# Hybrid encoder block: fourteen places for the expert weights instead of ten, and the last gate's weights sent through them

## The chip, the cores and the metric

The kernel runs on one core of a Trainium2 chip. The metric is the device time of one execution in microseconds (us). Engines are named as in the profile: PE (TensorE, matrix products), PEld (its weight loads), DVE (VectorE), ACT (ScalarE), POOL (GpSimd) and SP (SyncE, which here only issues transfers). MB in the text is 1,048,576 bytes, the size of one weight tile.

## What is computed

One layer of an encoder over 512 tokens of width 1024, all in float32. First a mixer of four branches with gates; then a mixture of 16 experts, in which each expert chooses 64 tokens; then a gate with an embedding; then a norm:

```
x = mixer_sublayer(x, ...)                       # four branches, gates, w_br, output projection w_out
x = x + expert_choice_ffn(rmsnorm(x, norm2_g), w_router, w_e_gate, w_e_up, w_e_down)
gate = sigmoid(rmsnorm(x, norm3_g) @ w_ple_gate)
x = x + gate * (p @ w_ple_proj)
return rmsnorm(x, final_g)

# expert e, on its 64 tokens xe
ye = (silu(xe @ w_gate[e]) * (xe @ w_up[e])) @ w_down[e]     # times the affinity, added to the tokens' rows
```

An expert's weights are 12 MB (gate and up 8 MB, down 4 MB), 192 MB for all; w_ple_gate is 4 MB.

## The kernel before

The program is one long list of instructions for each engine. It has four stretches: the branches with their gates, the output projection, the routing (eight rounds of a maximum search, and a gather of each expert's rows), and the experts with the last gate.

**Experts.** `up(e)` does eight steps k of four matmuls on the tile with the gate and up weights of k (L1213); then the activation (`gated`, L1216 and L1217); `hidden` transposes the result; `down(e)` does eight steps with the down weights, two steps to a tile (L1230). The order of PE is written out: after every second expert `spread` adds the results of a pair of experts to the tokens' rows X (L1255 to L1258), and a pair's rows are fetched (`fetch`, L1159) and transposed (`turn`). Experts 2 and 3 also carry parts of the embedding's projection (`project`, L1281), expert 12 the collection of the rows of the last two experts (`gather`). Tokens' results of experts 14 and 15 are finished apart.

**The last gate.** `base(i, k0, k1)` (four calls i of eight steps k) multiplies the tokens' rows with w_ple_gate. It does so in split precision: `gsplit(k, h)` makes from a 128x512 piece of the weights a rounded part gh on ACT and the rest gl on DVE (both through `parts`, L1092 and L1093), and PE takes six matmuls from them (L408 to L410). There are two buffers each for gh and gl, so step k+2 is split only when PE has left step k. `finish_gate` takes the same weights, not split, for the rows of experts 14 and 15.

**Places for weights.** A tile of 128 x 2048 numbers (1 MB) is given a place by `place()`: in rotation three of the pool `ring` (which held the weights of the earlier stretches) and seven of the pool `big`, which exists from the end of the output projection. The weights w_ple_gate have eight tiles `WG` of their own of 0.5 MB, loaded before the experts (L1087) and multiplied at once with the norm's gain g3 on ACT (L1088). Expert 0's down weights and the first step of expert 1 go to small tiles (`we`, 0.25 MB), which lie in the space of other, not yet needed buffers (the tags "x", "y" and "m").

All weights are issued by SP from one queue, in one order. SP waits with a transfer until PE has left the place's tile before, and everything behind it waits too. The lists below name a tile by `w`, whichever pool it is from.

Of the kernel before, what the change touches and what calls it, by code (L numbers as in the profile page):

```python
# [8 lines left out]
F32 = mybir.dt.float32  # L9
# [9 lines left out]
D = 1024  # L19
# [16 lines left out]
BIG = 14  # L36
# [7 lines left out]
KS = 4  # L44
WARM = 4
SOLO = (14, 15)
NEARLY = 8
FAR = 4096.0
SM = {}

# [155 lines left out]
def _body(ctx, tc, nc, A, out):  # L206
# [19 lines left out]
    def S(name, i=0):  # L226
        o, n = SM[name]
        return sm[:, o + i:o + i + 1]
# [53 lines left out]
    def YT(name, dt=F32R):  # L282
        return mpool.tile([128, 512], dt, name=name, tag="y", bufs=8)
# [609 lines left out]
    iap = xr.tile([128, 8], F32, name="iap")  # L893
    iai = xr.tile([128, 8], I32, name="iai")
    wr = xr.tile([128, 8, 16], F32, name="wr")
    wo = ctxR.enter_context(tc.tile_pool(name="wo", bufs=8, side="right", reuse_waits="tile"))

    def load_out(half):
# [29 lines left out]
    same = xl.tile([128, 64], F32, name="same")  # L928
    one = xl.tile([128, 128], F32, name="one")
    e6 = [xl.tile([128, 64], F32, name=f"e6{i}") for i in range(2)]  # L930
    WG = [xl.tile([128, D], F32, name=f"WG{k}") for k in range(8)]
    zp = ctx.enter_context(tc.tile_pool(name="zp", bufs=4, reuse_waits="tile"))
    h2d = dram.tile([T, D], F32, name="h2d")

# [88 lines left out]
                              ident.rearrange("p (c r) -> p r c", r=8)[:, 4 * h:4 * h + 4], start=True, stop=True)  # L1023
    ctxR.close()

    big = ctx.enter_context(tc.tile_pool(name="big", bufs=BIG // 2, side="right", reuse_waits="tile"))

    vals = xe[0:64, 256:384]
    idx = xe[0:64, 384:448].bitcast(U32)
# [53 lines left out]
    dve.tensor_copy(dsti[1], dst[1])  # L1083


    for k in range(8):
        sp.dma_start(WG[k], A["w_ple_gate"][k])  # L1087
        act.activation(WG[k], WG[k], AF.Copy, scale=S("g3", k))  # L1088

    def parts(hi, lo, v, eng=dve):  # L1090

        act.copy(hi, v)  # L1092
        eng.tensor_sub(lo, v, hi.bitcast(F32))  # L1093

    def xpart(b, i):

# [3 lines left out]
        xps[b, i] = MT("xTh", F32R), YT("xTl")  # L1100
        parts(*xps[b, i], p)

    nsplit = 0

    def gsplit(k, h, eng=dve):
        nonlocal nsplit
        if nsplit < 2:
            gh_.append((MT if nsplit else XH)("gh", F32R))
            gl_.append((MT if nsplit else XH)("gl", F32R))
        hi, lo = gh_[nsplit % 2], gl_[nsplit % 2]  # L1110
        nsplit += 1
        parts(hi, lo, WG[k][:, h * 512:(h + 1) * 512], eng)
        return hi, lo

    xps, Z, zb = {}, [], {}

    def base(i, k0, k1):
        bp, h = divmod(i, 2)
        if k0 == 0:
            zb[i] = [ps("b"), ps("b")]  # L1120
            if h == 0:
                z = place()
                Z.extend([z[:, 0:1024], z[:, 1024:2048]])
        for k in range(k0, k1):
            gh, gl = gsplit(k, h)
            for j in range(2):
                hi, lo = xps[2 * bp + j, k // 4]
                t = slice((k % 4) * 128, (k % 4 + 1) * 128)
                mm3(zb[i][j], hi[:, t], lo[:, t], gh, gl, k == 0, k == 7)
        if k1 == 8:  # L1130
            for j in range(2):
                act.copy(Z[2 * bp + j][:, h * 512:(h + 1) * 512], zb[i][j])
# [4 lines left out]
    n_w = 0  # L1137

    def place():
        nonlocal n_w  # L1140
        n_w += 1
        if n_w % (BIG // 2 + 3) < 3:
            t = ring.tile([128, 2048], F32, name="w", tag="w")
        else:
            t = big.tile([128, 2048], F32, name="w2", tag="w2")
        return t

    def wtile(src):
        t = place()
        sp.dma_start(t, src)  # L1150
        return t[:, 0:1024], t[:, 1024:2048]
# [23 lines left out]
    def halves(t):  # L1175
        return [t[:, 0:512], t[:, 512:1024]]

    def early(k):
# [4 lines left out]
            return [YT("we", F32), YT("we", F32)]  # L1183
        return [MT("we"), MT("we")]

    def load(e):
        wg, wu, wd = [], [], []
        for k in range(8):
            if e == 1 and k == 0:
                for i, w in enumerate((wg, wu)):  # L1190
                    w.append([YT("we", F32) for h in range(2)])
                    for h in range(2):
                        c = i * 1024 + h * 512
                        sp.dma_start(w[0][h], A["w_gu"][e, k, :, c:c + 512])
            else:
                for w, t in zip((wg, wu), wtile(A["w_gu"][e, k])):
                    w.append(halves(t))
        for k in range(8):
            if e == 0 and k < NEARLY:
                wd.append(early(k))  # L1200
                for h in range(2):
                    c = (k % 2) * 1024 + h * 512
                    sp.dma_start(wd[k][h], A["w_dn"][e, k // 2, :, c:c + 512])
            elif k % 2 == 0:
                wd.extend(halves(w) for w in wtile(A["w_dn"][e, k // 2]))
        return wg, wu, wd

    def up_part(e, xts, w2, acc, k0, k1):
# [75 lines left out]

    def project_rows():

        pg = MT("pg")
# [73 lines left out]
    def row_rstd(a, tag):  # L1361
# [3 lines left out]
            pe.matmul(q[:, 0:1], one, a[:, i:i + 1], start=i == 0, stop=i == 1)  # L1365
        return rstd(q[:, 0:1], 1.0 / D, tag=tag)


    def finish_start(x_, xgT, junk):

        for i in range(2):
            p = ps("t")
            s = slice(i * 256, (i + 1) * 256)
            for k in range(2 * i, 2 * i + 2):
                pe.transpose(p[:, k * 128:(k + 1) * 128], x_[:, k * 128:(k + 1) * 128], ident)
            act.copy(xgT[:, s], p[:, s])
        return row_sums(x_, "u", junk)

    def finish_factor(a):
# [63 lines left out]
    for b in range(2):  # L1443
        xpart(b, 0)
    up_part(14, xts, (wg, wu), acc, 2, 8)
    gated(acc)
    for b in range(2):
        xpart(b, 1)
    base(0, 0, 4)
# [106 lines left out]
```

## Time and profile before

| | us |
|---|---|
| median of 3 runs (range) | 1086.66 (1085.18 to 1088.04) |
| the profiled execution | 1086.17 |
| its span | 1084.4 |
| PE busy | 1004.5 (93%) |
| DVE, ACT busy | 482.3, 341.7 |
| mean granted PE clock | 0.982 of full speed |
| read from memory | 258.88 MB (10^6 bytes) |

The span is cut by the page into 40 slices of 27 us. PE is busy in tenths 8 to 9 nearly everywhere; around 520 to 548 us it waits for the routing. The weights' transfers keep the sixteen DMA engines full from about 520 us to about 1000 us; before that they are mostly idle.

### The profile page before, as it was taken

To read this page: it belongs to the slowest core of one execution; us is meant where nothing else is said; L and a number is where in the kernel's file an instruction comes from. 1 tells how busy PE (TensorE), PEld (TensorE's weight loads), DVE (VectorE), ACT (ScalarE), POOL (GpSimd) and SP (SyncE) were. 2 spreads that over 40 slices of the span, in tenths; PEclk is the share of its full clock that TensorE was granted. 3 is DMA by queue.
4 is the path that set the end of the run, shared out by engine and by line. 5 is a ranking of instruction groups with operands and counts; after the bars stand their busy time and mean duration, and the time that the engine had idled before them with its cause. 6 is when DMAs were issued, how large, how long until landed. Compare 5 with 4: busy or idle time off the path is not lost.

```text
span 1084.4 us, 12105 instructions
## 1 busy us (share of the span) xinstructions
PE 1004.5 (93%) x4566; PEld 597.4 (55%) x4566; DVE 482.3 (44%) x1078; ACT 341.7 (32%) x636; POOL 38.4 (4%) x45
## 2 busy tenths in 40 slices
PE   8999999999999999999489999988788898999996
PEld 5777887787668888878233333323232333336553
DVE  6996886555765556544600202011020203144646
ACT  6342335426553324362111111110101022134443
POOL 0022020000000000000000000000000000000001
PEclk9999999999999999999699999999999899999998
DMA  9222121411122532464998999999999999999401
GB/s 329 105 78 78 39 76 59 141 68 60 49 78 102 144 97 93 156 241 137 377 402 325 416 418 423 422 423 423 423 424 423 422 424 424 422 407 394 170 1 49
DMA packets 54259, 264.15 MB, mean 244 GB/s; under 512 B 6635, under 2 KB 11499, under 8 KB 30264
## 3 DMA queue, kind: packets, MB, share of 16 engines
q1 hardware_dynamic: 49840, 252.14, 58.8%
q0 software_dynamic: 1904, 6.44, 1.5%
q10 hardware_dynamic: 2456, 4.79, 1.4%
q8 instruction: 36, 0.59, 0.2%
q14 instruction: 23, 0.19, 0.1%
HBM read 258.88 MB, written 4.72 MB: 243 GB/s over the span
## 4 chain that ended last, share of the span: by engine, by line
PE 68%; DMA 15%; DVE 7%; issue 6%; ACT 3%; POOL 1%; POOLq 0%; SPq 0%; DVEq 0%; ACTq 0%
DMA w<-in_w_gu_dram 13%; PE ps_mm L1213 12%; PE ps_y L1230 8%; PE ps_mm L410 7%; PE ps_mm L409 7%; PE ps_mm L408 7%; PE ps_b L408 2%; PE ps_b L409 2%; PE ps_b L410 2%; PE ps_pj L408 2%; PE ps_pj L409 1%; PE ps_mm L990 1%; DVE X L1258 1%; PE ps_pj L410 1%; PE ps_mm L988 1%
## 5 line engine op out<-in xcount | busy, mean ns | idle before, releaser
L1213 PE MATMUL ps_mm<-w,xt 128*64 128x512 f32 x1016 | 230.8, 598 | 25.6 <-DMA w<-in_w_gu_dram 25.4
L1213 PEld LDWEIGHTS ps_mm<-w,xt 128*64 128x64 f32 x1016 | 70.8, 137 | 182.9 <-issue 121.3
L408 PE MATMUL ps_mm<-hhi,whi 128*128 128x512 f32 x392 | 156.7, 400 | 0.0
L410 PE MATMUL ps_mm<-hhi,wlo 128*128 128x512 f32 x392 | 155.2, 397 | 0.7 <-DVE wlo L325 0.5
L409 PE MATMUL ps_mm<-hlo,whi 128*128 128x512 f32 x392 | 154.9, 395 | 0.0
L1217 DVE TENSOR_TENSOR sg<-sg,ps_mm 128x512 f32<-128x512 f32 x16 | 11.0, 689 | 286.3 <-PE ps_mm L1213 286.3
L1230 PE MATMUL ps_y<-w,hd 128*64 128x512 f32 x480 | 109.2, 607 | 6.1 <-ACT hd L1238 6.1
L323 ACT CAST whi<-w 128x1024 fp32r<-128x1024 f32 x50 | 52.5, 1051 | 122.4 <-PE ps_mm L409 69.7
L408 PEld LDWEIGHTS ps_mm<-hhi,whi 128*128 128x128 f32 x392 | 74.1, 189 | 18.7 <-ACT whi L323 1.2
L410 PEld LDWEIGHTS ps_mm<-hhi,wlo 128*128 128x128 f32 x392 | 74.1, 189 | 18.7 <-issue 2.5
L409 PEld LDWEIGHTS ps_mm<-hlo,whi 128*128 128x128 f32 x392 | 74.0, 189 | 17.1 <-issue 2.5
L1216 ACT ACTIVATE sg<-ps_mm 128x512 f32<-128x512 f32 x16 | 9.6, 597 | 207.9 <-PE ps_mm L1213 207.9
L1230 PEld LDWEIGHTS ps_y<-w,hd 128*64 128x64 f32 x480 | 34.7, 139 | 70.8 <-issue 60.8
L325 DVE TENSOR_TENSOR wlo<-w,whi 128x1024 fp32r<-128x1024 f32 x49 | 60.1, 1230 | 5.9 <-ACT whi L323 5.8
L1248 ACT ACTIVATE ys<-ps_y,ia 64x512 f32<-64x512 f32 x28 | 19.1, 682 | 99.7 <-PE ps_y L1230 99.4
L1093 DVE TENSOR_TENSOR yh<-ys,yh 128x512 fp32r<-128x512 f32 x14 | 9.1, 688 | 76.2 <-ACT yh L1092 76.2
L621 DVE TENSOR_TENSOR sg<-ps_mm,rbs 128x512 f32<-128x512 f32 x32 | 22.1, 690 | 46.9 <-PE ps_mm L410 46.6
L1159 POOL DMA_INDIRECT xe<-h2d,iai x8 | 7.7, 966 | 712.3 <-DVE num L1081 373.4
L1093 DVE TENSOR_TENSOR gl<-WG,gh 128x512 fp32r<-128x512 f32 x32 | 22.1, 691 | 20.2 <-ACT gh L1092 20.2
L409 PE MATMUL ps_b<-gl,xTh 128*128 128x512 f32 x64 | 26.2, 410 | 0.6 <-DVE gl L1093 0.6
L1092 ACT CAST gh<-WG 128x512 fp32r<-128x512 f32 x32 | 19.9, 621 | 21.7 <-PE ps_b L410 15.5
L408 PE MATMUL ps_b<-gh,xTh 128*128 128x512 f32 x64 | 26.0, 406 | 0.0
(506 smaller groups left out, 1517.2 us busy)
## 6 DMA issues: line engine op xcount, KB each, us to landing
w<-in_w_gu_dram SPq DMA_DIRECT2D x127, 1024.0 KB, 19.2
w<-in_w_dn_dram SPq DMA_DIRECT2D x60, 1024.0 KB, 18.5
w<-in_w_in_dram SPq DMA_DIRECT2D x50, 512.0 KB, 4.1
wb<-in_w_br_dram SPq DMA_DIRECT2D x32, 128.0 KB, 2.2
w<-in_w_out_dram SPq DMA_DIRECT2D x8, 512.0 KB, 4.0
WG<-in_w_ple_gate_dram SPq DMA_DIRECT2D x8, 512.0 KB, 5.8
we<-in_w_dn_dram SPq DMA_DIRECT2D x16, 256.0 KB, 7.0
xk<-in_xT_dram SPq DMA_DIRECT2D x8, 256.0 KB, 3.9
```

Source lines behind the costliest of these rows:

```text
L323: act.copy(hi, raw)
L325: (pool if key in PW else dve).tensor_sub(lo, raw, hi.bitcast(F32))
L408: pe.matmul(p, whi, mhi, start=start, stop=False)
L409: pe.matmul(p, whi, mlo, start=False, stop=False)
L410: pe.matmul(p, wlo, mhi, start=False, stop=stop)
L621: dve.tensor_mul(g, p, rbs)
L1092: act.copy(hi, v)
L1093: eng.tensor_sub(lo, v, hi.bitcast(F32))
L1213: pe.matmul(t[h * 64:(h + 1) * 64], x, w[k][h], start=k == 0, stop=k == 7)
L1217: dve.tensor_mul(sg, sg, acc[1])
L1230: pe.matmul(y[h * 64:(h + 1) * 64], lt[:, k % 4, k // 4, :], w[k][h], start=n == 0, stop=n == 7)
L1248: act.activation(ys[h][r], y[hs], AF.Copy, scale=ia[hs, 16 + e:17 + e])
```

## The change

It makes fourteen places of ten. The eight WG tiles go; in their space lie four places (pool `wgp`). Of the seven places of `big` three become a pool `soon`, which is laid between the tokens' rows and the output projection's weights, in space that is free from the end of the branches; the other four stay in `big`. `place()` goes round all fourteen: wgp 0 to 3, ring 4 to 6, soon 7 to 9, big 10 to 13; a list TAIL gives the last ones by hand.

w_ple_gate is loaded as four tiles of 1 MB within expert 14's weights, between its up and its down weights. It is no longer multiplied by g3 beforehand: `gsplit` does it (an ACT activation with a scale for each row instead of a cast, and a DVE operation with that scale instead of a subtraction), and for the rows of experts 14 and 15 the transposed rows are multiplied instead (two DVE products in place of two ACT copies in `finish_start`). Two of expert 14's splits are made ahead of its activation.

Three more steps (2, k = 3, 4, 5) go to small tiles, as (1, 0) did, and the transfers after them are held behind them.

```diff
+AGAIN = {(1, 0): "y", (2, 3): "y", (2, 4): "m", (2, 5): "m"}
+N_ALL = 14 * 12 - 8 + 8 + 4
+TAIL = (4, 5, 6, 7) + (8,) + (9, 10, 11, 12, 13, 4, 5, 6) + (7, 9, 10, 11) + (12,)
+SOON = 3
...
+    soon = ctx.enter_context(tc.tile_pool(name="soon", bufs=SOON, side="right", reuse_waits="tile"))
     wo = ctxR.enter_context(tc.tile_pool(name="wo", bufs=8, side="right", reuse_waits="tile"))
...
-    WG = [xl.tile([128, D], F32, name=f"WG{k}") for k in range(8)]
+    wgp = ctx.enter_context(tc.tile_pool(name="wgp", bufs=4, reuse_waits="tile"))
...
-    big = ctx.enter_context(tc.tile_pool(name="big", bufs=BIG // 2, side="right", reuse_waits="tile"))
+    big = ctx.enter_context(tc.tile_pool(name="big", bufs=BIG // 2 - SOON, side="right", reuse_waits="tile"))
...
-    for k in range(8):
-        sp.dma_start(WG[k], A["w_ple_gate"][k])
-        act.activation(WG[k], WG[k], AF.Copy, scale=S("g3", k))
...
-        parts(hi, lo, WG[k][:, h * 512:(h + 1) * 512], eng)
-        return hi, lo
+        v = WG[k][:, h * 512:(h + 1) * 512]
+        i = act.activation(hi, v, AF.Copy, scale=S("g3", k))
+        dve.scalar_tensor_tensor(lo, v, S("g3", k), hi.bitcast(F32), op0=ALU.mult, op1=ALU.subtract)
+        return hi, lo, i
...
-        if n_w % (BIG // 2 + 3) < 3:
-            t = ring.tile([128, 2048], F32, name="w", tag="w")
-        else:
-            t = big.tile([128, 2048], F32, name="w2", tag="w2")
-        return t
+        pos = (n_w - 1) % 14 if n_w <= N_ALL else TAIL[n_w - N_ALL - 1]
+        if pos < 4:
+            return wgp.tile([128, 2048], F32, name="w3", tag="w3")
+        if pos < 7:
+            return ring.tile([128, 2048], F32, name="w", tag="w")
+        if pos < 7 + SOON:
+            return soon.tile([128, 2048], F32, name="w4", tag="w4")
+        return big.tile([128, 2048], F32, name="w2", tag="w2")
...
-            if e == 1 and k == 0:
+            if (e, k) in AGAIN:
+                T_ = YT if AGAIN[e, k] == "y" else MT
...
+        if e == 14:
+            for i in range(4):
+                t = place().rearrange("p (k d) -> p k d", k=2)
+                sp.dma_start(t, A["w_ple_gate"][2 * i:2 * i + 2].rearrange("k p d -> p k d"))
+                WG.extend([t[:, 0], t[:, 1]])
...
-            act.copy(xgT[:, s], p[:, s])
+            dve.tensor_mul(*(v[:, s].rearrange("p (a b c) -> p a b c", a=2, b=2) for v in (xgT, p)),
+                           g3[:, 2 * i:2 * i + 2].to_broadcast([128, 2, 2, 64]))
...
-    gated(acc)
+    ahead.extend(gsplit(k, 0) for k in range(2))
+    with tc.issue_after(ahead[1][2].ins):
+        gated(acc)
```

The first place is SP's queue after the output projection's weights (w_out). `w_gu` are gate and up weights, `w_dn` down weights. Before:

```order
L317 DMA w<-in_w_out_dram 128x1024 x7
L1150 DMA w<-in_w_gu_dram 128x2048
L1087 DMA WG_4116<-in_w_ple_gate_dram 128x1024
...
L1087 DMA WG_4123<-in_w_ple_gate_dram 128x1024
L1150 DMA w<-in_w_gu_dram 128x2048 x2
L1203 DMA we<-in_w_dn_dram 128x512 x4
L1194 DMA we<-in_w_gu_dram 128x512 x3
L1150 DMA w_4751<-in_w_gu_dram 128x2048
```

And now:

```order
L321 DMA w<-in_w_out_dram 128x1024 x7
L1157 DMA w<-in_w_gu_dram 128x2048
L1157 DMA w_4729<-in_w_gu_dram 128x2048
...
L1157 DMA w_4735<-in_w_gu_dram 128x2048
L1157 DMA w<-in_w_gu_dram 128x2048 x2
L1219 DMA we<-in_w_dn_dram 128x512 x4
L1204 DMA we<-in_w_gu_dram 128x512 x4
L1157 DMA w_4851<-in_w_gu_dram 128x2048
```

Where the eight gate tiles stood, four tiles of expert 0 stand. Three more tiles (expert 0's last step, expert 1's second and third) go out earlier still, on SP among the loads of the gates, behind the tokens' rows X. Before:

```order
L915 DMA X_3268<-in_x_dram 128x1x1024
L317 DMA w<-in_w_in_dram 128x1024
L612 DMA wb<-in_w_br_dram 128x256
L317 DMA w<-in_w_in_dram 128x1024
L612 DMA wb<-in_w_br_dram 128x256
```

And now:

```order
L920 DMA X_3268<-in_x_dram 128x1x1024
L1157 DMA w_4743<-in_w_gu_dram 128x2048
L616 DMA wb<-in_w_br_dram 128x256
L321 DMA w<-in_w_in_dram 128x1024 x2
L1157 DMA w_4847<-in_w_gu_dram 128x2048
L616 DMA wb<-in_w_br_dram 128x256
L1157 DMA w_4849<-in_w_gu_dram 128x2048
```

Three loads of 1 MB now stand between the gates' loads, which are otherwise as they were.

The second place is the end of SP's queue, from expert 14's last up tile on. Before, its down weights follow at once:

```order
L1150 DMA w_6456<-in_w_gu_dram 128x2048
L1150 DMA w<-in_w_gu_dram 128x2048 x2
L1150 DMA w<-in_w_dn_dram 128x2048
L1150 DMA w_6464<-in_w_dn_dram 128x2048
...
L1150 DMA w<-in_w_gu_dram 128x2048
L1150 DMA w_6798<-in_w_gu_dram 128x2048
```

Now the last gate's weights stand between, and expert 15's tiles behind them:

```order
L1157 DMA w_6460<-in_w_gu_dram 128x2048
L1212 DMA w_6462<-in_w_ple_gate_dram 128x2x1024
...
L1212 DMA w_6468<-in_w_ple_gate_dram 128x2x1024
L1157 DMA w<-in_w_dn_dram 128x2048 x3
L1157 DMA w_6476<-in_w_dn_dram 128x2048
L1157 DMA w_6806<-in_w_gu_dram 128x2048
```

So 4 MB have moved from before expert 0 to within expert 14; the order of PE among the experts is as it was.

## Rows read from the trace of the kernel before

**Rows 1.** The page's slices of 27 us: busy share of the DMA engines, GB/s

```profile
DMA  9222121411122532464998999999999999999401
GB/s 329 105 78 78 39 76 59 141 68 60 49 78 102 144 97 93 156 241 137 377 402 325 416 418 423 422 423 423 423 424 423 422 424 424 422 407 394 170 1 49
```

**Rows 2.** PE's waits, 545 to 1075 us: total us, times, longest

```profile
PE ps_mm L1213 <- DMA w<-in_w_gu_dram: 25.4, 40, 1.7
```

**Rows 3.** Stretches: length, busy us (instructions) of PE, PEld, DVE, ACT, POOL; clock, DMA share, GB/s

```profile
360.00:380.00 20.00, 20.00 (x90) 16.46 (x89) 11.51 (x24) 5.73 (x10) 0.00 (x0) 1.00 0.68 178
...
480.00:490.00 10.00, 10.00 (x49) 7.96 (x48) 6.46 (x10) 10.00 (x18) 0.00 (x0) 1.00 0.36 130
...
575.00:580.00 5.00, 5.00 (x26) 1.72 (x24) 0.00 (x0) 0.00 (x0) 0.00 (x0) 1.00 0.39 123
...
628.00:630.00 2.00, 2.00 (x12) 0.72 (x10) 0.00 (x0) 0.00 (x0) 0.00 (x0) 1.00 0.99 389
...
680.00:700.00 20.00, 18.55 (x90) 7.07 (x86) 0.69 (x1) 2.05 (x4) 0.00 (x0) 1.00 1.01 424
...
880.00:900.00 20.00, 16.47 (x78) 5.49 (x76) 2.38 (x4) 4.76 (x8) 0.94 (x1) 1.00 1.01 423
```

**Rows 4.** SP's issues in order: start, us to the last one, line, transfer, count

```profile
460.93 16.73 SPq L1087 DMA_DIRECT2D WG<-in_w_ple_gate_dram  x8
486.10 3.55 SPq L1150 DMA_DIRECT2D w<-in_w_gu_dram  x2
...
526.01 16.50 SPq L1203 DMA_DIRECT2D we<-in_w_dn_dram  x12
...
612.75 15.01 SPq L1150 DMA_DIRECT2D w<-in_w_gu_dram  x4
...
625.72 0.33 SPq L1150 DMA_DIRECT2D w<-in_w_gu_dram  x1
```

**Rows 5.** From issue to landing: the tile issued at 612.75, then two at 577 to 579

```profile
DMA to landing us min/median/max: 13.8/13.8/13.8
...
DMA to landing us min/median/max: 4.8/5.5/6.1
```

**Rows 6.** PE in order: start, us, line, operation, count, idle before

```profile
545.00 1.07 PE L1169 MATMUL ps_t<-ident,xe 128*128 128x128 f32 x8 [3.79 <-DMA xe<-h2d,iai]
...
600.53 13.90 PE L1213 MATMUL ps_mm<-w,xt 128*64 128x512 f32 x64
...
623.74 7.09 PE L1230 MATMUL ps_y<-w,hd 128*64 128x512 f32 x32 [0.72 <-ACT hd L1238]
...
909.79 1.94 PE L1213 MATMUL ps_mm<-w,xt 128*64 128x512 f32 x8 [0.55 <-DMA w<-in_w_gu_dram]
...
931.47 13.90 PE L1213 MATMUL ps_mm<-w,xt 128*64 128x512 f32 x64
...
965.78 10.52 PE L1213 MATMUL ps_mm<-w,xt 128*64 128x512 f32 x48
...
979.48 0.50 PE L409 MATMUL ps_b<-gl,xTh 128*128 128x512 f32 x1 [0.41 <-DVE gl L1093]
...
989.77 7.09 PE L1230 MATMUL ps_y<-w,hd 128*64 128x512 f32 x32
```

**Rows 7.** Splits, x32 and x8: ns min/median/max, first and last start, shape

```profile
L1092 ACT CAST gh<-WG x32: 603/621/632, 948.9 to 1063.2; 128x512 fp32r<-128x512 f32 x32
L1093 DVE TENSOR_TENSOR gl<-WG,gh x32: 681/693/694, 949.6 to 1063.9; 128x512 fp32r<-128x512 f32 x32
...
L358 ACT ACTIVATE hhi<-xk,sm x8: 707/724/727, 4.7 to 13.4; 128x512 fp32r<-128x512 f32 x8
...
L359 DVE SCALAR_TENSOR_TENSOR hlo<-xk,sm,hhi x8: 745/747/753, 5.5 to 14.7; 128x512 fp32r<-128x512 f32 x8
```

**Rows 8.** PE in the last gate's second call: two matmuls of one step

```profile
999.88 0.50 PE L409 MATMUL ps_b<-gl,xTh 128*128 128x512 f32 x1
1000.22 0.39 PE L410 MATMUL ps_b<-gh,xTl 128*128 128x512 f32 x1
```

More of the change, by code (lines that the diff above doesn't have):

```diff
@@ L46 @@
 SOLO = (14, 15)
-NEARLY = 8
+AGAIN = {(1, 0): "y", (2, 3): "y", (2, 4): "m", (2, 5): "m"}
+N_ALL = 14 * 12 - 8 + 8 + 4
+TAIL = (4, 5, 6, 7) + (8,) + (9, 10, 11, 12, 13, 4, 5, 6) + (7, 9, 10, 11) + (12,)
+SOON = 3
 FAR = 4096.0
@@ L1083, in _body, with parts @@
     dve.tensor_copy(dsti[1], dst[1])
-    for k in range(8):
-        sp.dma_start(WG[k], A["w_ple_gate"][k])
-        act.activation(WG[k], WG[k], AF.Copy, scale=S("g3", k))
-    def parts(hi, lo, v, eng=dve):
+    def parts(hi, lo, v):
         act.copy(hi, v)
-        eng.tensor_sub(lo, v, hi.bitcast(F32))
+        dve.tensor_sub(lo, v, hi.bitcast(F32))
     def xpart(b, i):
@@ L1101, in xpart, with gsplit @@
         parts(*xps[b, i], p)
-    nsplit = 0
-    def gsplit(k, h, eng=dve):
+    nsplit, ahead = 0, []
+    def gsplit(k, h):
         nonlocal nsplit
@@ L1111, in gsplit @@
         nsplit += 1
-        parts(hi, lo, WG[k][:, h * 512:(h + 1) * 512], eng)
-        return hi, lo
-    xps, Z, zb = {}, [], {}
+        v = WG[k][:, h * 512:(h + 1) * 512]
+        i = act.activation(hi, v, AF.Copy, scale=S("g3", k))
+        dve.scalar_tensor_tensor(lo, v, S("g3", k), hi.bitcast(F32), op0=ALU.mult, op1=ALU.subtract)
+        return hi, lo, i
+    xps, Z, zb, WG = {}, [], {}, []
     def base(i, k0, k1):
@@ L1124, in base @@
         for k in range(k0, k1):
-            gh, gl = gsplit(k, h)
+            gh, gl = (ahead.pop(0) if ahead else gsplit(k, h))[:2]
             for j in range(2):
@@ L1184, in early @@
         return [MT("we"), MT("we")]
+    early_ = []
     def load(e):
@@ L1188, in load @@
         for k in range(8):
-            if e == 1 and k == 0:
+            if (e, k) in AGAIN:
+                T_ = YT if AGAIN[e, k] == "y" else MT
                 for i, w in enumerate((wg, wu)):
-                    w.append([YT("we", F32) for h in range(2)])
+                    w.append([T_("we", F32) for h in range(2)])
                     for h in range(2):
                         c = i * 1024 + h * 512
-                        sp.dma_start(w[0][h], A["w_gu"][e, k, :, c:c + 512])
+                        early_.append(sp.dma_start(w[k][h], A["w_gu"][e, k, :, c:c + 512]))
             else:
-                for w, t in zip((wg, wu), wtile(A["w_gu"][e, k])):
-                    w.append(halves(t))
+                with tc.issue_after(early_[-1].ins) if e == 2 and k > 5 or e == 3 else nullcontext():
+                    for w, t in zip((wg, wu), wtile(A["w_gu"][e, k])):
+                        w.append(halves(t))
+        if e == 14:
[3 more added lines that the diff above has]
+                WG.extend([t[:, 0], t[:, 1]])
         for k in range(8):
-            if e == 0 and k < NEARLY:
+            if e == 0:
                 wd.append(early(k))
@@ L1204, in load @@
             elif k % 2 == 0:
-                wd.extend(halves(w) for w in wtile(A["w_dn"][e, k // 2]))
+                with tc.issue_after(early_[-1].ins) if e == 2 else nullcontext():
+                    wd.extend(halves(w) for w in wtile(A["w_dn"][e, k // 2]))
         return wg, wu, wd
@@ L1285, in project_rows @@
     def project_rows():
-        pg = MT("pg")
+        pg = XH("pg")
         pool.indirect_dma_start(out=pg[:, 0:256], out_offset=None, in_=A["p"],
@@ L1366, in row_rstd @@
         return rstd(q[:, 0:1], 1.0 / D, tag=tag)
+    g3 = sm[:, SM["g3"][0]:SM["g3"][0] + 8].rearrange("p (b a c) -> p a b c", b=2, c=1)
     def finish_start(x_, xgT, junk):
```

## The prediction

> **What bounds the kernel now.** I read the slices of the page first, then PE's waits, then the stretches with the share of the DMA engines, then SP's issues against PE's order. From about 540 us the memory delivers at one flat rate [rows 1]: 424 GB/s in every stretch of 20 us between 640 and 900 us, of which two are shown [rows 3]. So one tile of 1 MB costs 1.0486 / 0.424 = 2.47 us, and a pair of experts (24 tiles and a fetch of 0.5 MB) 60.6 us. PE alone needs less: unhindered, the up matmuls of one expert take 13.9 us [rows 6], where at 2.47 us a tile eight steps take 19.8. That is why PE's idle time before L1213 is 25.4 us in 40 small pieces [rows 2]: the wait is spread over the steps of the experts from about 680 us to expert 12, whose last up tile is waited for at 909.79 [rows 6]. Behind it nothing waits for a weight: the up matmuls of expert 13 run in 13.90 us, the rest of expert 14's in 10.52 for 48 [rows 6]. So what counts is when the stream of tiles brings expert 12's last up tile, number 12 x 12 + 8 = 152; all behind it shifts with that.
>
> When does that tile come? The engines are full without a break, so the answer hangs on the last moment at which the stream stood still for want of a place. Those moments can be seen. From 575 to 580 us the DMA share falls to 0.39 [rows 3]: expert 0's down weights hold no place of the ring, so PE frees none while it uses them. The last one is in expert 2. Its up matmuls end at 600.53 + 13.90 = 614.43, its down matmuls begin at 623.74 [rows 6]; between them lie the spread and the projection, which free nothing. SP issued a tile at 612.75 and the next only at 625.72 [rows 4]. The former landed 13.8 us after its issue [rows 5], at 626.55, while a tile issued into a nearly dry queue needs 4.8 us [rows 5], of which 2.47 are its data; the one of 625.72 thus came a little late, and the rate dips to 389 GB/s [rows 3]. From there the backlog only grows. The tile issued at 625.72 is number 43 (three experts and seven). The 109 tiles from it to number 152 set the clock of the experts.
>
> **The change part by part.**
>
> *Four places more.* The release that let tile 43 go now lets go the tile that lies four further on, number 47: fourteen places after the same tile instead of ten. If the stream is still held by that release, everything behind comes 4 x 2.47 = 9.9 us earlier. It is held: by the time of the routing it is further ahead than four tiles. Before, 3 tiles had been issued by 490 us (one at 450, two from 486.10 on), beside the eight gate tiles, 16.73 us of issues from 460.93 [rows 4]; now the gate tiles' 4 MB are four expert tiles, and three more go out during the gates, so it is 10. Of these 7 tiles of lead (17.3 us) the places can hold only four when PE reaches expert 2. So I take -9.9 us; the ends are 0 (the lead is lost elsewhere) and -17.3 (all of it lasts).
>
> Can PE follow? It waits 25.4 us for up tiles in all [rows 2], so 9.9 can be taken away, and some 15 stay. Waiting should begin about two experts later than now.
>
> One rule speaks otherwise on the rate. The row shows 424 GB/s [rows 3]. The Trainium skill (DMA: Bandwidth & Descriptors, section "Where 436 GB/s comes from") says that for transfers from HBM about 358 GB/s per core binds; by that four tiles would be worth an estimated 11.7 us. The trace differs, and the measured rate stands.
>
> *The small tiles.* Steps 3 to 5 of expert 2 need no place; their buffers are free once expert 0's down matmuls are done, some 30 us before use. They are used up before the release of 625 us, so they add nothing to the lead. 0 us.
>
> *The early tiles.* Three loads of 1 MB among the gates' loads: DMA share 0.68 or less there, PE busy 20.00 of 20 us [rows 3], loads of the gates issued several tiles ahead. Three tiles are 7.4 us of transfer, and the gates' loads behind them have more lead than that. 0 us; were it not hidden, up to 7.4.
>
> *The routing.* PE waits 3.79 us for the first fetch of rows [rows 6], which shares the engines with the stream. Before, 12 tiles were queued for 511 to 545 us, now 9, so the last of them may be gone when the fetch runs. Between 0 and -3.8; I take -0.7, near the end at 0, since the h2d stores and the small tiles still fill most of that time.
>
> *Scaling on ACT removed.* Eight products between 474 and 490 us: PE was busy 10.00 of 10 us there [rows 3], so 0.
>
> *The gate's weights in the stream.* Tiles 177 to 180 are now w_ple_gate. On the clock of before, tile 177 lands 25 x 2.47 + 1.2 (a fetch) = 63 us after tile 152, at 973; expert 14's up matmuls end at 965.78 + 10.52 = 976.30 [rows 6]. The splits take 1.3 us a piece: about 2 us to spare. After it 0.5 MB (1.24 us) comes for every step of six matmuls (about 1.4 us). Expert 14's first down tile, now 181, lands at 983, needed at 989.77 [rows 6]. 0 us, with the cover named: expert 12's and 14's work without weights.
>
> *The splits.* The cast is 621 ns, the subtraction 693 [rows 7]. The nearest rows for their successors are the same shapes at the start: 724 on ACT and 747 on DVE [rows 7], together 0.157 us more. It matters, because two buffers make a loop: PE leaves step k, ACT and DVE split k+2, PE needs it at the second matmul of k+2. The matmul of 999.88 starts 0.34 us before the next instead of 0.23 [rows 8]: the loop is already the limit, by 0.11 us in about every second step. I count ten such places in the four calls: 10 x 0.157 = +1.6 us. Bounds: 0, and 32 x 0.157 = +5.0 if each split were in series. Against it, two splits are made ahead, so the stall before 979.48 (0.41 us idle, and the half filled gap before) goes: -0.7 us.
>
> *finish_start.* Two DVE products of 128x256 for two ACT copies: neither is on PE's path; +-0.4, taken as 0.
>
> Sum: -9.9 - 0.7 + 1.6 - 0.7 = -9.7. The profiled execution took 1086.17 us, so 1076.5; that is as far below the median of 1086.66 to half a microsecond.
>
> **The rivals.**
>
> *The whole lead lasts.* If the places were no limit at expert 2, 7 tiles x 2.47 = 17.3 us: 1086.2 - 17.3 + 0.2 (the other terms) = 1069. For it: the stall at 575 to 580 is the greatest and vanishes. Against it: the gap in releases from 614 to 625 stays as it is.
>
> *The gate's weights eat the gain.* The 4 MB were loaded when the engines had room; now they are in the full stretch and cost 9.9 us. If the stream is more than 2 to 3 us later at expert 14 than I work out, PE waits for tile 177 and each one after it, and the places' gain is paid back in part or whole: 1083 to 1089.
>
> *The splits become the bound, slower.* The same mechanism, with the last gate's loop at its dear end: the gain of 9.9 paid back by the 9.9 of the gate's tiles, and all 32 splits in series at +5.0: 1086.2 + 5.0 = 1091. It decides where both ACT and DVE come late to each step, that is where gh waits for its weights too. Against it: the 7 us that expert 14's down weights have in hand.
>
> *Small pieces.* Twelve pieces of 0.25 MB took 16.50 us of issuing [rows 4], 9.1 us more than 3 tiles at 2.47. Should the three steps of expert 2 pay that, the lead of 7 tiles shrinks by 9.1 us to 8.2, 1.7 short of the four that can be held: 1078, within the range. The Trainium skill (DMA: Bandwidth & Descriptors, section "Measured (HBM→SBUF, 128 partitions, SWDGE, issued from GpSimd)") advises 1 MiB or more to a transfer, which speaks for this rival.
>
> **How the numbers follow.** Forecast 1076.5, itself 1072 to 1081 (fetch at its gaining end, splits at 3 to 4 us, small pieces): 0.70. The whole lead, 1066 to 1071: 0.12. Paid back, 1083 to 1089: 0.11. Slower, near 1091: 0.07. The range takes the first two and the near end of the third: 1068 to 1082. A measurement tells about 0.3% (3.3 us) from no change; so faster 0.82, same 0.11, slower 0.07.
>
> **What would show it.** Right: the DMA share below 1 around 615 to 625, where it now is full; PE's first wait for an up tile at expert 7 or 8 instead of 5 or 6; the last at expert 12, at about 899; about 15 us of waits in L1213 instead of 25.4; no wait for w in the last gate; gh near 0.72 us, gl near 0.75, with steps of about 1.5 us each in the last gate. Wrong: waits that end at expert 9 or earlier (the whole lead), PE idle on w_ple_gate after expert 14's up (paid back), or gaps before L409 in every step beyond 0.2 us.

## The result, and the profile after

The changed kernel took **1074.12 us** (median; 1072.60 to 1077.42), the kernel before it, on the same chip, 1085.92 us (1083.71 to 1088.04): a ratio of **0.9896**, 95% interval 0.9865 to 0.9927, so 11.8 us less. That is faster by the bound of 0.3%, 2.4 us under the forecast and inside its range. The profiled execution, 1077.42 us with a span of 1075.6, was the longest of the four.

The slices of the page answer to [rows 1]. Each is 27 us; the first line is the busy share of the DMA engines, the second what they moved:

```profile
DMA  9322121322122653463879989999999999999601
GB/s 313 125 79 79 40 71 65 102 80 83 54 79 78 202 178 99 157 237 103 313 299 406 424 339 425 424 425 425 425 426 424 424 424 428 422 410 425 260 1 50
```

The plateau is there again at 424 to 426 GB/s, but now with a notch: 339 GB/s in the 24th slice, about 618 to 645 us, where before it was flat. The three stretches around it say where (columns as in [rows 3]):

```profile
615.00:620.00 5.00, 5.00 (x22) 2.94 (x18) 3.78 (x7) 0.60 (x1) 0.00 (x0) 1.00 1.00 424
620.00:625.00 5.00, 4.22 (x13) 1.94 (x12) 1.69 (x3) 1.31 (x3) 0.00 (x0) 1.00 0.72 305
625.00:630.00 5.00, 4.59 (x22) 1.63 (x24) 0.00 (x0) 0.36 (x1) 0.00 (x0) 1.00 0.33 97
```

The memory now stands still for some 4.8 us (0.28 and 0.67 of 5 us) in expert 2, because all places are taken. SP's issues show the other side of it (columns as in [rows 4]): seven early tiles in one row from 451.83, and in expert 2 four issues of expert 3's down tiles drawn out over 15 us, where before the same happened to four up tiles:

```profile
451.83 39.08 SPq L1157 DMA_DIRECT2D w<-in_w_gu_dram  x7
...
614.43 15.01 SPq L1157 DMA_DIRECT2D w<-in_w_dn_dram  x4
```

PE's waits between 535 and 1070 us, which answer to [rows 2] (total, times, longest):

```profile
PE ps_mm L1230 <- DMA w<-in_w_gu_dram: 17.1, 28, 1.8
...
PE ps_t L1176 <- DMA xe<-h2d,iai: 2.2, 1, 2.2
```

And PE in order, which answers to [rows 6]: expert 0's first matmul, the first wait for an up tile (expert 7's last step), and the last one (expert 12's):

```profile
549.49 10.92 PE L1230 MATMUL ps_mm<-w,xt 128*64 128x512 f32 x48
...
748.04 1.94 PE L1230 MATMUL ps_mm<-w,xt 128*64 128x512 f32 x8 [0.56 <-DMA w<-in_w_gu_dram]
...
899.41 1.94 PE L1230 MATMUL ps_mm<-w,xt 128*64 128x512 f32 x8 [0.49 <-DMA w<-in_w_gu_dram]
```

**Where the time went.** Three marks cut an execution into parts that can be compared: SP's issue of two halves of w_in shortly before 350 us (the same code in all kernels; call it A), expert 0's first up matmul (S), and the start of the matmuls on expert 12's last up tile (L). The table is worked out from the starts in the traces; all times in us.

| kernel | A | S - A | L - S | end of span - L |
|---|---|---|---|---|
| before | 345.89 | 201.82 | 362.08 | 174.61 |
| after | 347.44 | 202.05 | 349.92 | 176.19 |
| difference | +1.55 | +0.23 | **-12.16** | +1.58 |

The sum is -8.8 us, the difference of the two spans. The first column is no effect: A lies between 344.9 and 347.4 in all the profiled executions below, in code that is the same. The early tiles behind A delay nothing: from A to POOL's issue of the first fetch of rows it is 192.12 us before and 192.09 after. The gain sits where the prediction put it, between S and L, and part of it is given back behind L.

### The profile page after: what moved, and what is told of

Its sections match the earlier page's. It is cut to its first block, busy times and chain, and to the rows that moved or that the text cites. A ratio compares the mean times of both kernels' runs of the same rounds, so it can differ in the third digit from the quotient of the medians.

```text
span 1075.6 us, 12115 instructions
## 1 busy us (share of the span) xinstructions
PE 1004.6 (93%) x4566; PEld 601.4 (56%) x4566; DVE 485.4 (45%) x1082; ACT 336.5 (31%) x624; POOL 38.4 (4%) x45
## 4 chain that ended last, share of the span: by engine, by line
PE 71%; DMA 17%; DVE 7%; ACT 2%; issue 2%; POOL 0%; POOLq 0%; SPq 0%; DVEq 0%; ACTq 0%
PE ps_mm L1230 12%; DMA w<-in_w_gu_dram 11%; PE ps_y L1247 8%; PE ps_mm L414 8%; PE ps_mm L413 8%; PE ps_mm L412 7%; DMA w<-in_w_dn_dram 4%; PE ps_b L412 3%; PE ps_b L413 3%; PE ps_b L414 3%; PE ps_pj L412 2%; PE ps_pj L413 1%; PE ps_mm L995 1%; PE ps_pj L414 1%; PE ps_mm L993 1%
## 5 line engine op out<-in xcount | busy, mean ns | idle before, releaser
L1230 PE MATMUL ps_mm<-w,xt 128*64 128x512 f32 x992 | 222.5, 596 | 17.1 <-DMA w<-in_w_gu_dram 17.1
L1115 DVE SCALAR_TENSOR_TENSOR gl<-w,sm,gh 128x512 fp32r<-128x512 f32 x32 | 24.0, 751 | 21.8 <-ACT gh L1114 21.7
L1114 ACT ACTIVATE gh<-w,sm 128x512 fp32r<-128x512 f32 x32 | 23.0, 723 | 28.0 <-PE ps_b L414 20.4
L626 ACT ACTIVATE sg<-sg,hbg 128x512 f32<-128x512 f32 x32 | 23.1, 721 | 12.8 <-DVE sg L625 12.8
```

The lines of the kernel that those rows point to most:

```text
L626: act.activation(g, g, AF.Tanh, bias=hbg[:, n * 8 + d:n * 8 + d + 1], scale=0.5)
L1114: i = act.activation(hi, v, AF.Copy, scale=S("g3", k))
L1115: dve.scalar_tensor_tensor(lo, v, S("g3", k), hi.bitcast(F32), op0=ALU.mult, op1=ALU.subtract)
L1230: pe.matmul(t[h * 64:(h + 1) * 64], x, w[k][h], start=k == 0, stop=k == 7)
```

## The experiments

The theory at the start was the prediction's: the place that comes free in expert 2 sets the stream's clock, each place more is one tile, and nothing else counts. All kernels are the changed one with the edit shown. Of each profiled execution the same marks:

| kernel | places | S - A | L - S | end - L | wait for the first fetch | median us (ratio to before on the same chip) |
|---|---|---|---|---|---|---|
| before | 10 | 201.82 | 362.08 | 174.61 | 3.8 | 1085.92 |
| after | 14 | 202.05 | 349.92 | 176.19 | 2.2 | 1074.12 (0.9896) |
| e1_again | 14 | 202.13 | 349.82 | 176.43 | 3.9 | 1076.01 (0.9890) |
| e2_twelve | 12 | 198.58 | 355.00 | 175.40 | none | 1075.78 (0.9896) |
| e3_soon_late | 14 | 203.36 | 349.24 | 176.14 | 4.6 | 1076.29 (0.9901) |
| e4_no_gate_load | 14 | 202.60 | 349.12 | 176.12 | 2.6 | 1074.47 (0.9878) |
| e5_hold | 14, held | 198.60 | 349.20 | 175.48 | 1.4 | 1070.69 (0.9867) |
| e6_third_split | 14 | 202.90 | 349.05 | 178.86 | 2.6 | 1077.88 (0.9919) |
| e7_plain_split | 14 | 200.88 | 348.87 | 174.61 | 3.3 | 1073.33 (0.9892) |
| e8_no_small | 14 | 200.61 | 350.43 | 175.57 | 3.2 | 1075.63 (0.9909) |
| e9_hold_again | 14, held | 198.73 | 348.76 | 175.58 | 1.3 | 1071.81 (0.9870) |
| e10_unheld | 14 | 200.51 | 349.21 | 175.60 | 1.8 | 1074.29 (0.9890) |
| e11_twelve_again | 12 | 198.37 | 355.24 | 175.47 | 1.3 | 1077.13 (0.9912) |
| e12_hold_third | 14, held | 198.86 | 349.07 | 176.11 | 0.3 | 1071.45 (0.9864) |

Held means that some tiles are kept behind the first fetch (e5_hold below). The 95% intervals of the ratios reach 0.0015 to 0.0025 to either side (some 1.6 to 2.7 us). e1 to e4 share a chip and its runs of before, so do e5 to e8, and e9 to e12. Medians are compared within such a group where no other is named.

**e1_again**, the changed kernel unedited, the measure for e2 to e4.

> The changed kernel once more, on the chip that runs the next three, as the value they are held against. Both theories: 1074 us, between 1072.5 and 1077.5, and expert 12's last up tile lands at 898 to 900 us of its span.

It took 1076.01 us (1074.11 to 1076.60), and expert 12's last up tile was started on at 898.37.

**e2_twelve**: two of the late places fewer (the order of the last places is fitted to twelve).

```diff
-    big = ... bufs=BIG // 2 - SOON, ...
+    big = ... bufs=BIG // 2 - SOON - 2, ...
-        pos = (n_w - 1) % 14 if n_w <= N_ALL else TAIL[n_w - N_ALL - 1]
+        pos = (n_w - 1) % 12 if n_w <= N_ALL else TAIL[n_w - N_ALL - 1]
```

> Twelve places of 1 MB in place of fourteen: two of the seven late ones are left out, the three early ones and all early issues stay. Theory of the places (what counts is how many tiles may be under way when a place next comes free, in expert 2): the same release now lets tile 45 go instead of tile 47, so expert 12's last up tile lands 2 x 2.47 = 4.9 us later, at 903 to 905 us, and the time is 1079 us, +5 (4 to 6) over the changed kernel of this call. Rival, the early lead of seven tiles is what the change brought: the early issues are untouched, so the difference is under 1 us.

1075.78 us (1075.52 to 1076.81): no difference, as the rival had it, and the last up tile at 898.50. Taken alone this would have ended the theory. The traces say otherwise. PE in order in e1_again, the transposes of the fetched rows, two products, expert 0's first matmul and the last wait:

```profile
545.74 1.17 PE L1176 MATMUL ps_t<-ident,xe 128*128 128x128 f32 x8 [3.92 <-DMA xe<-h2d,iai]
546.70 1.92 PE L1298 MATMUL ps_pj<-wpp,pT 128*128 128x512 f32 x2
548.55 11.65 PE L1230 MATMUL ps_mm<-w,xt 128*64 128x512 f32 x50
...
898.37 1.94 PE L1230 MATMUL ps_mm<-w,xt 128*64 128x512 f32 x8 [0.49 <-DMA w<-in_w_gu_dram]
```

The same four in e2_twelve:

```profile
541.64 1.07 PE L1176 MATMUL ps_t<-ident,xe 128*128 128x128 f32 x8
542.55 1.02 PE L1298 MATMUL ps_pj<-wpp,pT 128*128 128x512 f32 x2
543.50 13.95 PE L1230 MATMUL ps_mm<-w,xt 128*64 128x512 f32 x64
...
898.50 1.94 PE L1230 MATMUL ps_mm<-w,xt 128*64 128x512 f32 x8 [0.55 <-DMA w<-in_w_gu_dram]
```

With twelve places no wait for the fetch is left, where there were 3.92 us, and PE begins the experts 3.55 us sooner (198.58 against 202.13 behind A). Of these, 2.60 us are the fetch: the transposes begin 196.72 us behind A instead of 199.32. The other 0.95 us is PE's granted clock, 0.66 in the 5 us behind the wait in e1_again, where the two products then take 1.92 us instead of 1.02. From there to the last up tile PE needs 5.18 us longer (355.00 against 349.82), and the two nearly cancel. Why the fetch comes sooner is seen in the stretches around it. First e1_again, then e2_twelve:

```profile
535.00:540.00 5.00, 4.34 (x9) 2.29 (x10) 2.84 (x19) 0.21 (x1) 1.14 (x1) 0.52 0.96 345
540.00:545.00 5.00, 1.82 (x5) 0.51 (x3) 0.00 (x0) 1.19 (x2) 0.00 (x0) 1.00 1.01 408
545.00:550.00 5.00, 4.26 (x14) 1.87 (x16) 0.00 (x0) 2.41 (x3) 0.96 (x1) 0.66 0.35 105
```

```profile
535.00:540.00 5.00, 5.00 (x8) 2.23 (x8) 2.62 (x18) 0.60 (x1) 1.14 (x1) 0.50 0.47 143
540.00:545.00 5.00, 4.96 (x21) 2.10 (x21) 0.00 (x0) 2.95 (x4) 0.96 (x1) 0.92 0.28 79
```

With fourteen places there is room for two more tiles of 1 MB at 534 us; the engines are full (1.01) when the fetch runs, and PE stands (1.82 us busy of 5). With twelve the places are used up, the engines half idle (0.47, 0.28), and the fetch passes: from its issue to the transposes it is 4.57 us, in e1_again 7.18. (The length of the wait alone does not tell this, since PE's four products ahead of it took 2.98 us in e2_twelve and 1.88 in e1_again. In e11_twelve_again below, PE waits 1.29 us and S - A is no longer.) So there are two mechanisms. The release in expert 2 is PE's own doing: it comes when PE has used expert 2's first down tile, 77.5 us after S. In e2_twelve SP's issue shows that moment:

```profile
344.92 0.80 SPq L321 DMA_DIRECT2D w<-in_w_in_dram  x2
...
621.00 5.48 SPq L1157 DMA_DIRECT2D w<-in_w_dn_dram  x4
```

621.00 is 77.5 after 543.50 (623.00 after 545.49 in e11_twelve_again, 77.5 as well); in the kernel before the tile of 625.72 [rows 4] went 78.0 after its S of 547.71, and in after the tile of 627.39 went 77.9 after 549.49. What makes PE late ahead of the experts makes the whole stream late.

**e3_soon_late**: the three places that exist from the branches' end are made behind the output projection.

```diff
-    soon = ctx.enter_context(tc.tile_pool(name="soon", bufs=SOON, ...))
     wo = ctxR.enter_context(...)
 ...
     ctxR.close()
+    soon = ctx.enter_context(tc.tile_pool(name="soon", bufs=SOON, ...))
```

> The three places that exist from the branches' end are made only with the seven late ones, behind the output projection; fourteen places as in the changed kernel. Theory of the places: the queue that issues them still runs into the stall in expert 2 with all fourteen taken, and the tile that the release there lets go is the same one; 0 to +1 us (1074 to 1075), and the stall ahead of 625 us gets shorter or goes. Rival, the early lead: three tiles of the lead are gone, 3 x 2.47 = +7.4 us, 1081.5 us.

1076.29 us (1075.49 to 1077.22), +0.3 beside e1: the theory; the three early issues bring nothing on their own. One part of the expectation was wrong. The stall was to get shorter, and it did not:

```profile
620.00:625.00 5.00, 4.28 (x17) 1.88 (x17) 0.13 (x1) 1.67 (x3) 0.00 (x0) 1.00 0.40 165
625.00:630.00 5.00, 5.00 (x26) 1.67 (x24) 0.00 (x0) 0.00 (x0) 0.00 (x0) 1.00 0.61 218
```

0.60 and 0.39 of 5 us are 4.95 us of stillness, in e1_again (shares 0.60 and 0.42) 4.9. The lead of three tiles is lost before expert 2: in e1_again the engines already have a pause at 545 to 555 us (shares 0.35 and 0.69), in e3 none there (1.04 and 1.09).

**e4_no_gate_load**: the four last tiles that carry w_ple_gate are not loaded; tiles of expert 13 that are still in their places are used in their stead, so the kernel leaves out the gate's part of the output.

```diff
-                t = place().rearrange("p (k d) -> p k d", k=2)
-                sp.dma_start(t, A["w_ple_gate"][2 * i:2 * i + 2]...)
-                WG.extend([t[:, 0], t[:, 1]])
+            for t in kept:
+                WG.extend([t[:, 0:1024], t[:, 1024:2048]])
```

> The 4 MB of the last gate's weights are not loaded; the four tiles of expert 13 that stand in those places earlier are kept and used in their stead, so the gate's part of the output is left out and the stream is four tiles shorter at its end. Theory of the places: the gate's first tile is there about 1.5 us before the engine that splits it could begin, and the stream's end has no other waiter: 0 to -1.5 us. Rival, the gate's weights inside the stream take a part of the gain back: -3 to -9.9 us, the whole of four tiles.

1074.47 us (1071.59 to 1076.18), -1.5 beside e1: at the edge of the theory's range and short of the rival's. L - S and the part behind L are those of the unedited kernel to less than 1 us (349.12 and 176.12; after had 349.92 and 176.19, e10 349.21). In the trace of after ACT waits for the gate's first tile, but PE does not wait for ACT:

```profile
964.36 1.33 ACT L1114 ACTIVATE gh<-w,sm 128x512 fp32r<-128x512 f32 x2 [6.73 <-DMA w<-in_w_ple_gate_dram]
965.87 0.60 ACT L1233 ACTIVATE sg<-ps_mm 128x512 f32<-128x512 f32 x1 [0.17 <-PE ps_mm L1230]
```

Two splits of 1.33 us end at 965.69, and the next ACT work, expert 14's activation, is PE's to release, 0.17 us later. The gate's tiles come just in time; the cover is thin.

**e8_no_small**: expert 2's up steps 3 to 5 in three ordinary places instead of twelve small pieces; the order of the places is shifted to fit, and the transfers that were held behind the small pieces are not held.

```diff
-AGAIN = {(1, 0): "y", (2, 3): "y", (2, 4): "m", (2, 5): "m"}
+AGAIN = {(1, 0): "y"}
```

> Expert 2's up steps 3 to 5 through three ordinary places instead of twelve small pieces in buffers of their own. Theory of the places: the same 3 MB pass in the same order, but they now take places, so the release in expert 2 lets a tile go that is three nearer the front, +3 x 2.47 = +7.4 us at most, and PE's start is sooner by up to 3.5 us because the stream stops ahead of the fetch: +4 to +7.4 us, 1080 to 1083.5 beside 1076. Rival, the small pieces only move bytes and the places are no limit: 0.

1075.63 us, L - S of 350.43 and S - A of 200.61: nothing like +4 to +7.4. The expectation read the theory wrongly: the three tiles move the tile that waits by three, and the place it waits for as well, since they lie in front of both. SP's issues are drawn out over the same four tiles, as long as ever:

```profile
610.34 15.01 SPq L1157 DMA_DIRECT2D w<-in_w_dn_dram  x4
```

The memory, though, hardly stood still here: the DMA share is 0.93 from 625 to 630 us, where after has 0.33, and the tile that the release let go landed 6.0 us after its issue instead of 4.6. L - S is 0.5 to 1.7 us longer than in the others with fourteen places. The prediction's 0 for the small tiles fits the time; the trace gives them about 1 us.

**e5_hold**: if the fetch's wait delays the release, the tiles that stand ahead of it have to go behind it, with all fourteen places kept. A write of two columns by POOL, queued behind the fetch, holds expert 1's up tile 5 and what SP has behind it.

```diff
+        if behind:
+            with tc.issue_after(g0.ins):
+                pool.memset(t[:, 0:2], 0.0)
         sp.dma_start(t, src)
 ...
-                    for w, t in zip((wg, wu), wtile(A["w_gu"][e, k])):
+                    for w, t in zip((wg, wu), wtile(A["w_gu"][e, k], (e, k) == (1, 5))):
```

> The changed kernel, with expert 1's up tile 5 and what the queue has behind it held until the first fetch of routed rows is issued (a two-column write by POOL behind that fetch, into the tile's place); fourteen places as before. Theory, formed on the run with twelve places: the last place-limited release is PE's own doing, and PE stands 3 to 4 us late because the fetch of its rows lies behind two tiles of 1 MB. Without them PE begins expert 0 about 3.5 us sooner, the release in expert 2 and expert 12's last up tile come as much sooner, and the time is 3 to 4 us under the changed kernel's: 1072 us beside its 1076. Rival, the stream's own lost time counts: two tiles are 5 us late, and expert 12's last tile comes at the same time or up to 5 us later: 1076 to 1081 us.

1070.69 us (1069.95 to 1072.42), ratio 0.9867 with an interval of 0.9850 to 0.9884. PE in order:

```profile
541.66 1.06 PE L1179 MATMUL ps_t<-ident,xe 128*128 128x128 f32 x8 [1.36 <-DMA xe<-h2d,iai]
...
543.52 7.95 PE L1233 MATMUL ps_mm<-w,xt 128*64 128x512 f32 x36
...
892.72 1.94 PE L1233 MATMUL ps_mm<-w,xt 128*64 128x512 f32 x8 [0.48 <-DMA w<-in_w_gu_dram]
```

S stands where twelve places had it (198.60 behind A), and L - S is that of fourteen (349.20). The rival, that two tiles 5 us late would show at the end, falls: the stretches show the idle time at the fetch, and the stall in expert 2 still there, so the stream had time to lose.

```profile
535.00:540.00 5.00, 5.00 (x9) 2.06 (x9) 2.62 (x18) 0.60 (x1) 1.26 (x2) 0.67 0.57 189
...
615.00:620.00 5.00, 4.28 (x17) 1.84 (x17) 0.32 (x1) 1.67 (x3) 0.00 (x0) 1.00 0.38 159
620.00:625.00 5.00, 5.00 (x26) 1.68 (x24) 0.00 (x0) 0.00 (x0) 0.00 (x0) 1.00 0.62 203
```

The hold did less than was meant: of the two tiles one still went out ahead of the fetch, at 531.75 (the fetch's issue is at 537.01); the other went at 538.29, and four pieces of 0.25 MB behind it, 2 MB in all. With that one tile ahead the fetch is nearly as quick as with none: 4.65 us from its issue to the transposes, in e2_twelve 4.57.

**e9_hold_again, e10_unheld, e11_twelve_again**: the held kernel, the changed kernel and the one with twelve places, side by side on one chip. Held and twelve have the same S to 0.4 us, so but for the hold itself they differ by two places.

> The kernel with the two tiles held behind the first fetch of rows once more, beside the three that follow on the same chip. Theory (place-limited release plus the tensor engine's own start): expert 0 begins 198.6 us after the queue's first early issue and expert 12's last up tile 349.3 us after that; 3 to 4 us under the unheld kernel of this call, about 1071. Rival (the gain of the first look came from the chip or the clock): within 1 us of the unheld kernel.

> The changed kernel as it is, on the same chip as the held one. Theory and rival: 1074 to 1076.5 us, expert 0's start 202 us after the queue's first early issue, expert 12's last up tile 349.3 us after expert 0's start.

> Twelve places once more. Its tensor engine starts expert 0 where the held kernel's does (198.6 us after the queue's first early issue in both), so beside the held kernel it differs by the two places alone. Theory of the places: expert 12's last up tile 355 us after expert 0's start, 2 x 2.6 = 5.2 us behind the held kernel's, and the time 4.5 to 6 us over it: 1076. Rival (places beyond twelve bring nothing): the same as the held kernel.

1071.81 us (1069.74 to 1073.93), 1074.29 (1071.14 to 1076.69) and 1077.13 (1076.03 to 1078.01). **Two places are worth 5.3 us**, with ranges that do not touch; the rival of e11 falls. Between S and L they are 6.5 us (355.24 against 348.76). The held kernel lies 2.5 us under the unheld one, less than the 3 to 4 expected, and the ranges overlap. In this unheld execution S - A was 200.51, in the seven unheld ones with fourteen places beside it (after, e1, e3, e4, e6, e7 and e8) 200.6 to 203.4. The spread is mostly PE's clock: from the fetch's issue to the transposes it is 6.5 to 7.7 us in all eight, but from the transposes to S it is 1.86 us in e7, e8 and e10 and 2.8 to 3.5 in the other five, where the granted clock fell behind the wait (0.66 to 0.76 from 545 to 550 us). Holding takes both away: 4.65 to 4.87 us, then 1.86, and S - A of 198.6 to 198.9 in all three.

**e7_plain_split**: the splits of before, without the gain.

```diff
-        i = act.activation(hi, v, AF.Copy, scale=S("g3", k))
-        dve.scalar_tensor_tensor(lo, v, S("g3", k), hi.bitcast(F32), op0=ALU.mult, op1=ALU.subtract)
+        i = act.copy(hi, v)
+        dve.tensor_sub(lo, v, hi.bitcast(F32))
```

> The splits of the gate's weights without the gain: a plain copy and a plain subtraction, as in the kernel before; the gain g3 is left out of the gate's product. Theory of the splits: 10 periods at 0.165 us come back, -1.6 us (0 to -2), a period of two steps falls from 3.02 to 2.86 us. Rival, the splits are covered: 0, and the period stays.

The time, 1073.33 us at a ratio of 0.9892, can't tell 1.6 us from nothing. The trace can: behind L it needs 174.61 us, where the four others that had the clock event told of in the last section (after, e1, e3, e4) needed 176.12 to 176.43, so 1.5 to 1.8 less. In the gate's second call the 15 intervals between the first products of its 16 half steps take 10.80 us (982.70 to 993.50) instead of 11.29 in e9_hold_again (979.10 to 990.39).

**e6_third_split and e12_hold_third**: a third pair of buffers for the splits, out of a place that is free by then, from the sixteenth split on, and in e12, on the held kernel, from the eighteenth.

```diff
+        if nsplit == 18:
+            z = place()
+            gh_.append(z[:, 0:512].bitcast(F32R))
+            gl_.append(z[:, 512:1024].bitcast(F32R))
-        hi, lo = gh_[nsplit % 2], gl_[nsplit % 2]
+        n = nsplit % 2 if nsplit < 18 else (nsplit - 16) % 3
+        hi, lo = gh_[n], gl_[n]
```

> A third pair of buffers for the split gate weights from the sixteenth split on. Theory of the splits (each pair of steps is 0.165 us longer by the dearer split, since the next split waits for a buffer): in the last two of the four products the engines' waits on each other go, a period of two steps falls from 3.02 to about 2.75 us, 8 x 0.27 = 2.2 us less at most and 1.2 us if only half of it lies on the path: 1073.8 to 1074.8 beside 1076. Rival, the tensor engine sets the pace there: 0.

> The held kernel with a third pair of buffers for the split gate weights from the eighteenth split on, when the place that it takes has long been read; in the earlier try the place came free 1.4 us after it was wanted and the tensor engine ran several products at its lower clock. Theory of the splits (two pairs of buffers cost 3.02 - 2.76 = 0.26 us in two steps): 7 pairs of steps, -1 to -1.8 us beside the held kernel, 1069 to 1070. Rival, another hand sets the pace (ACT between the splits, or the products themselves): 0.

e6 took 1077.88 us, slower than the unedited kernel in any group. The new pair's place was that of an up tile of expert 15, and the first split into it, made ahead in the other kernels, stood on ACT only at 1019.31 us. PE in order:

```profile
1020.07 0.50 PE L412 MATMUL ps_b<-w,xTh 128*128 128x512 f32 x1 [1.42 <-ACT w L1119]
1021.20 0.80 PE L413 MATMUL ps_b<-w,xTh 128*128 128x512 f32 x1 [0.63 <-DVE w L1120]
1021.79 0.63 PE L414 MATMUL ps_b<-w,xTl 128*128 128x512 f32 x1
```

Two waits, 2.05 us together, and then products at 0.63 us instead of 0.39, the lower clock. e12, with that mended, took 1071.45 us beside 1071.81: no difference. In the last call of the gate the first eight half steps do go faster, 4.94 us (1038.74 to 1043.68) instead of 5.23 (1036.67 to 1041.90), but in the call before it the first split into the new pair again comes late:

```profile
1015.72 0.51 PE L413 MATMUL ps_b<-w,xTh 128*128 128x512 f32 x1 [0.60 <-DVE w L1120]
```

Whether a third pair that is there from the start would pay wasn't tried.

## Why the prediction was right, step by step

- **The bound: right. The place where it is set: right for the changed kernel, misread in the kernel before.** The stream of up tiles to expert 12, its last place-limited moment in expert 2, the notch at 620 to 630 us, PE's first wait at expert 7, the last at 899.41, 17.1 us of waits where some 15 were named: all as put for the changed kernel, and e11 beside e9 shows that places are what counts. In the kernel before, the row of 612.75 [rows 4] holds four issues, and the last one ahead of tile 43 was not that of 612.75 but the next, at 614.47:

```profile
614.47 11.58 SPq L1150 DMA_DIRECT2D w<-in_w_gu_dram  x2
...
DMA to landing us min/median/max: 15.3/15.3/15.3
...
625.00:630.00 5.00, 5.00 (x26) 1.72 (x24) 0.00 (x0) 0.00 (x0) 0.00 (x0) 1.00 1.01 408
```

  So that tile landed at 629.8, some 4 us after tile 43 was issued at 625.72, and the engines had no pause. Tile 43 did not come late: the stream was still behind from its pause at 575 to 580 us [rows 3]. Here the first line holds the issue of that tile and of tile 43, the second is the former's time to landing, the third a stretch.
- **Four places: right in kind, too small.** -9.9 forecast, -12.2 measured between S and L. The mis-sized term has two parts. The smaller is the price of a tile. The plateau's rate gives 2.47 us, but the stream also carries the fetched rows and small loads: from the landing of the released tile to the start on expert 12's last one it took (899.41 - 631.98) / 105 = 2.55 us a tile after, and (898.50 - 626.92) / 107 = 2.54 with twelve places. Four tiles at 2.54 are 10.2 us. The larger part is the misreading above. In after the tile let go by the release found the engines idle and landed 4.6 us after its issue, with twelve places after 5.9 and 6.1 us. Tile 43 of the kernel before needed some 6.6 us; this is an estimate, since its own landing is not in the trace, from that of the tile behind it (634.79) less 2.5. These 2.0 us come on top of the four tiles: with fewer places the release was not the only thing that held the stream. Together 12.2. The plateau's rate is 424 to 426 GB/s in the trace of after. The Trainium skill (DMA: Bandwidth & Descriptors, section "Where 436 GB/s comes from") has some 358 as what binds; the trace differs in after as it did before, and that 11.7 us, the estimate by it, lies near the 12.2 is chance.
- **The whole lead lasts: the rival fell,** by e3: three early tiles less cost 0.3 us.
- **The routing: the step that failed,** by what it left out more than by its number. It was taken as a small term of its own (-0.7), and S - A came out 0.2 us longer. It is no term of its own, since the release that sets the stream is counted from PE's start: what delays PE ahead of the experts delays the end. With fourteen places there is room for two tiles ahead of the fetch that twelve do not have (in the kernel before, with ten places and another order of transfers, the engines were full at the fetch too: 6.99 us from its issue to the transposes). And the wait can cost PE's clock as well, up to 1.7 us more before S. So the two mechanisms are coupled, and e2 would have told a wrong story without its marks.
- **Small and early tiles: 0, right** in the times (e8, e3); for the small ones the trace has about 1 us.
- **The gate's weights in the stream: 0, right** (e4), but of the forecast 2 us to spare next to nothing was left: the splits of the first tile ended 0.17 us before ACT was wanted. Neither the rival of paid-back gain nor the slower one came.
- **The splits: +1.6, right** (e7: 1.5 to 1.8). The page of after has the two operations at the durations taken from [rows 7]:

```profile
L1115 DVE SCALAR_TENSOR_TENSOR gl<-w,sm,gh 128x512 fp32r<-128x512 f32 x32 | 24.0, 751 | 21.8 <-ACT gh L1114 21.7
...
L1114 ACT ACTIVATE gh<-w,sm 128x512 fp32r<-128x512 f32 x32 | 23.0, 723 | 28.0 <-PE ps_b L414 20.4
```

- **The rest behind L.** In executions without the clock event it is 175.5 us against 174.6 before, so of the 1.6 of the splits 0.7 came back, as much as the two splits made ahead were to bring; that this is the cause was not tried. The clock event, +0.7, was not foreseen.

The sum was -9.7, and the medians moved by -11.8. Without the column A the profiled executions differ by 10.4 us: the places gave 2.3 more than forecast, the routing 0.9 less, and the clock event took 0.7. That the sum came so near is in part these errors cancelling.

## What to carry to other kernels

When a stream runs full behind its last stall for a place, a place more is worth one tile of the stream at its real spacing (count from the released tile's landing to the start on the last one waited for, all traffic included: 2.54 us here, not 2.47), and the places at that stall count, not the tiles loaded ahead of it. Before a release is called the bound, look whether the tile ahead of it had landed: where it had not, an earlier stall still holds the stream, and a place is worth more. The release is an engine's doing, so look for what delays that engine earlier: here a small transfer that the whole chain waits for lay behind 3 MB that nobody needed yet, and with 2 MB of them held back the median was 2.5 us lower (e9 beside e10, ranges overlapping) and PE's start 1.8 us sooner. Where two effects can cancel, compare marks inside the execution and not the totals.

## What the runs showed of the hardware

Not expected was that TensorE's granted clock fell in the gather of expert 12, in some executions and not in others, with the same waits ahead of it. The stretches in e1_again:

```profile
904.00:908.00 4.00, 2.29 (x11) 1.17 (x9) 4.00 (x12) 3.20 (x6) 0.00 (x0) 1.00 1.01 426
908.00:912.00 4.00, 4.00 (x11) 2.89 (x10) 3.64 (x7) 1.95 (x4) 0.00 (x0) 0.57 1.01 426
```

Before the fall PE had been idle for 1.19 and 0.51 us among short products; at 0.57 of full speed on average a product of 0.40 us takes 0.63, which is the lower of the two levels (1.2 and 2.4 GHz) for most of that stretch. e2_twelve has the same two waits, 1.19 and 0.51 us, and its products stay at 0.40 to 0.50. Among the kernels with the new splits and two pairs of buffers, the part behind L is 176.1 to 176.4 us where it falls and 175.4 to 175.6 where it does not: 0.7 us. The same shows at the first fetch: behind a wait of 1.8 to 4.6 us the clock fell in before, after, e1, e3, e4 and e6, and not in e7, e8 and e10. What decides it was not found in either place.
